# Modulation portions of the second layer's mixer at even distances in TensorE's order

## The chip, the cores and the metric

One Trainium2 chip, one core. The time is device microseconds (us) of one launch of the program, from its runs on the chip; lower is better. The engines are named as in the profile: PE (TensorE, matrix multiplication), PEld (its weight loads), DVE (VectorE), ACT (ScalarE), POOL (GpSimd), SP (SyncE, here the queue that issues most DMAs).

## The reference

Two transformer layers (`DEPTH = 2`) over 256 tokens `x` and 256 context tokens, width 1024, all in float32. Each layer takes six modulation vectors from the condition, runs a mixer (a gated recurrence, neighbourhood attention and windowed attention with a sink), and a mixture of 16 experts. In the last layer only the 256 tokens of `x` go on behind the mixer.

```python
def ada_mod(cond, w, b):
    m = (jax.nn.silu(cond) @ w + b)[..., None, :]
    return jnp.split(m, 6, axis=-1)

for l in range(DEPTH):
    last = l == DEPTH - 1
    sh1, sc1, g1, sh2, sc2, g2 = ada_mod(c, w_ada[l], b_ada[l])
    csh1, csc1, cg1, csh2, csc2, cg2 = ada_mod(c_ctx, w_ada[l], b_ada[l])
    h = x * (1.0 + sc1) + sh1
    hc = ctx * (1.0 + csc1) + csh1
    y, yc = mixer(h, hc, w_in[l], ..., w_out[l], not last)
    x = layer_norm(alpha * x + g1 * y, ln1_g[l], ln1_b[l])
    h2 = x * (1.0 + sc2) + sh2
    ...
    f = moe(h2.reshape(-1, d), w_router, router_bias, w_gate[l], w_up[l], w_down[l]).reshape(x.shape)
    x = layer_norm(alpha * x + g2 * f, ln2_g[l], ln2_b[l])
```

## The kernel before

Every float32 product with a large weight is made of three fast products: a weight piece is split into a high part (a cast on ACT, L294) and a low part (a subtraction on DVE, L304), and the tokens are kept as high and low parts in the regions A, B and C. The split weights go in turn into the regions S and T, so a projection of 128 columns (`proj`, L432) is 24 matrix multiplications out of S or out of T, and the next piece can be split into a region only when the projection before last has read it.

The second layer's mixer (`mixer(1)`) is a set of Python generators that `weave` steps in turn. A rate says how many steps a generator makes in a round. The rounds only say in which order instructions are put into the program; a scheduler then orders each engine's instructions by that order, by priorities and by when it expects their operands. On the chip each engine follows its own order strictly. There are three weaves in this mixer, called the first, second and third window below:

- first: projections (`proj`), the neighbourhood attention of two head pairs (`ux(0, 1)`, `heads_x`), and portions of modulation (`fills(n[0])`);
- second: the recurrence of the first head pair (`hgrn(1, 0)`), projections, `fills(n[1])`;
- third: the recurrence of the second head pair (`hgrn(1, 1)`), projections, windowed attention (`ux(2, 3)`), `fills(n[2])`.

Behind them come the last attention heads woven with the output projection (`outproj`, `op` in the rows, L727), the layer norm, the router and the experts.

A portion of modulation (`fill`, then `ada`) makes two of the 24 blocks of `w_ada`. Its two weight pieces of 1 MB are loaded by POOL (L404) into the two buffers of `aring`, so the pieces of one portion can be loaded only when the portion before has read its own. Then follow 2 x 16 matrix multiplications on PE (`ada`, L411, 32 columns wide, so four stand side by side in the array), a copy on ACT (`vt`, L414), four transposes on PE (`adaT`, L417), and a reduction and two additions on DVE (L419, L424). When the last block of a layer is there, `vectors` makes the router's scaled weights on DVE (L664 to L679, L684), one small product on PE (`rb`, L683), and writes four vectors to DRAM over ACT's queue (`vd`, L687); SP loads them back (L690), and the layer norm's first multiplication (L800) takes the first of them. The portions are made in a fixed order: 14 in the first layer, 6 in the second, here called portions 1 to 6.

`heads_x` makes scores (`S`, L1117), subtracts maxima on DVE (L1122, L1125, L1127), exponentials on ACT (L1129), scales by the sums on DVE (L1137), transposes on PE (`pt`, L1140), copies on ACT (L1141), and multiplies by the values (`py`, L1147). `hgrn` makes seven groups of products on 128 x 128 blocks (`lev`, L999), each behind multiplications on DVE (L1029 to L1032, L989), then transposes of its keys (`kT`, L1049), state products (`dS`, L1056), outputs (`oT`, L1074, L1077) and a norm (`rms`, L1082).

The accumulators are PSUM banks of two pools: three ("d") for `proj`, `pt`, `py`, `kT` and others by `BANKS`, five ("m") for the rest, `ada`, `adaT`, `S`, `lev` and `rb` among them.

```python
FILLS = ((4, 5, 4, 1), (3, 2, 1, 0))
RATES = ((1, 2, 1, 2, 1, 1, 1, 1, 1, 1, 1, 2, 1, 1, 1, 2),
         (1, 2, 2, 2, 1, 1, 1, 1, 2, 3, 1, 1, 1, 1, 1, 3))
```

`FILLS[1]` gives the portions of each call site of the second layer, `RATES[1]` the rates (entries 2, 6 and 10 are those of `fills`).

Of the kernel before, what the change touches and what calls it, by code (L numbers as in the profile page):

```python
# [41 lines left out]
BANKS = {"proj": "d", "first1": "d", "first5": "d", "op1": "d", "xtp": "d", "nT1": "d", "rot": "d", "kT": "d",  # L42
         "pt": "d", "py": "d", "pos": "d", "hgt": "d", "hT": "d", "lt0": "d"}
SPLITC = 6
FILLS = ((4, 5, 4, 1), (3, 2, 1, 0))
EARLY = 6
TAILS = (4, 2)
BANKS1 = {"gu": "d", "hgt": "d", "dn": "m", "hT": "m", "sl": "m"}
ACC = "mmmd"
RATES = ((1, 2, 1, 2, 1, 1, 1, 1, 1, 1, 1, 2, 1, 1, 1, 2),  # L50
         (1, 2, 2, 2, 1, 1, 1, 1, 2, 3, 1, 1, 1, 1, 1, 3))
PRIO = {"hgrn": 0, "x": 200, "c": 0, "op": 0, "ln": 30}

C_ID, C_BLK, C_ROT = 0, 128, 256
# [136 lines left out]
class _Builder:  # L191
# [340 lines left out]
    def mixer(self, l):  # L532
# [48 lines left out]
        def fills(n):  # L581
            for _ in range(n):
                self.fill()
                yield

        def weave(*gs):
            live = list(gs)
# [17 lines left out]
        self.aring = [self.E[2], self.E[3]]  # L605
        n = FILLS[l]
        r = RATES[l]
        self.have.update(COLS[l][:6 + 2 * l])
        weave((pj(6 + 2 * l, 12), r[0]), (ux(0, 1), r[1], "x"), (fills(n[0]), r[2]))
        if l == 0 and not self.general:  # L610
            self.Yd = self.dram([2 * NT, D], "Yd0")
            self.behind(nc.vector.memset(self.Sd, 0.0), self.lasts[1])
            for i in range(2 * NT * D // (512 * P)):
                nc.sync.dma_start(self.Yd[:, :].rearrange("(p r) d -> p (r d)", p=P)[:, i * 512:(i + 1) * 512], self.Sd)
        weave((self.hgrn(l, 0), r[3], "hgrn"), (pj(12, 16), r[4]), (uc(0, 1), r[5], "c"), (fills(n[1]), r[6]))
        for _ in pj(16, 17):
            pass
        weave((self.hgrn(l, 1), r[7], "hgrn"), (pj(17, 22), r[8]), (ux(2, 3), r[9], "x"), (fills(n[2]), r[10]))
        self.direct = True
        cs = range(1 if last else 2)  # L620
# [1604 lines left out]
```

## Time and profile before

| | |
|---|---|
| time, median of 3 runs | 1170.52 us |
| lowest and highest of them | 1166.29 and 1172.93 us |
| the profiled execution's own time | 1173.01 us |
| its span, first to last instruction | 1171.0 us |
| PE busy in the span | 1072.6 us (92%) |
| DVE busy | 744.6 us (64%) |
| ACT busy | 527.1 us (45%) |
| POOL busy | 127.8 us (11%) |
| second layer's mixer, from portion 1 to the end of the output projection | 744.7 to 911.7 us |

The span is that of one execution under the profiler. A row of the timeline gives the start in the span, the time in us, the engine, the source line, the operation, out<-in, the shape and the number of instructions merged into the row; in brackets stands how long the engine sat idle before, and what ended that. Matrix multiplications overlap each other, so the starts of consecutive rows tell more than their times. A short wait of some hundredths of a microsecond is not printed. Rows of stretches (A:B) give for each engine the busy time and, in brackets, the instructions, then the clock that was granted to PE (1.00 is the full 2.4 GHz), the share of the DMA engines and their rate.

### The profile page before, as it was taken

To read this page: it belongs to the slowest core of one execution; us is meant where nothing else is said; L and a number is where in the kernel's file an instruction comes from. 1 tells how busy PE (TensorE), PEld (TensorE's weight loads), DVE (VectorE), ACT (ScalarE), POOL (GpSimd) and SP (SyncE) were. 2 spreads that over 40 slices of the span, in tenths; PEclk is the share of its full clock that TensorE was granted. 3 is DMA by queue.
4 is the path that set the end of the run, shared out by engine and by line. 5 is a ranking of instruction groups with operands and counts; after the bars stand their busy time and mean duration, and the time that the engine had idled before them with its cause. 6 is when DMAs were issued, how large, how long until landed. Compare 5 with 4: busy or idle time off the path is not lost.

```text
span 1171.0 us, 18720 instructions
## 1 busy us (share of the span) xinstructions
PE 1072.6 (92%) x7041; PEld 701.6 (60%) x7041; DVE 744.6 (64%) x1703; ACT 527.1 (45%) x872; POOL 127.8 (11%) x136
## 2 busy tenths in 40 slices
PE   5999999999995999999999968999999499999994
PEld 3776766665674777677644458667766444544451
DVE  3456687767689899788723586578786842222224
ACT  2363443437553677678633354543456511111113
POOL 0000011100000133334310000001000000000000
PEclk8999999999996799999999989999999699999997
DMA  9757666653366799799999951555528579999993
GB/s 376 261 210 263 261 225 233 232 194 127 126 246 237 242 358 358 276 362 384 368 406 415 408 205 72 180 181 216 181 71 332 200 283 422 420 423 422 421 422 155
DMA packets 55202, 327.14 MB, mean 279 GB/s; under 512 B 9467, under 2 KB 9723, under 8 KB 19776
## 3 DMA queue, kind: packets, MB, share of 16 engines
q1 hardware_dynamic: 44080, 275.60, 61.0%
q0 software_dynamic: 9152, 50.10, 11.5%
q8 instruction: 57, 0.93, 0.3%
q10 hardware_dynamic: 1872, 0.16, 0.1%
q14 instruction: 41, 0.34, 0.1%
HBM read 316.53 MB, written 13.09 MB: 281 GB/s over the span
## 4 chain that ended last, share of the span: by engine, by line
PE 74%; DVE 14%; ACT 4%; DMA 3%; issue 3%; POOL 1%; SPq 0%; DVEq 0%; ACTq 0%; POOLq 0%
PE proj L432 13%; PE gu L185 9%; PE gu L1647 7%; PE dn L185 4%; PE dn L1647 4%; PE op L727 4%; PE gu L1638 4%; PE first L432 3%; DMA G<-in_w_ada_dram 3%; PE ada L411 3%; PE pt L1140 2%; PE acc L185 2%; PE hgt L185 2%; PE dn L1638 2%; PE S L1117 2%
## 5 line engine op out<-in xcount | busy, mean ns | idle before, releaser
L294 ACT CAST S<-G 128x1024 fp32r<-128x1024 f32 (+2 forms) x83 | 79.3, 959 | 83.1 <-PE proj L432 52.9
L294 ACT CAST T<-G 128x1024 fp32r<-128x1024 f32 (+2 forms) x79 | 78.1, 994 | 85.0 <-PE proj L432 56.1
L304 DVE TENSOR_TENSOR S<-G,S 128x1024 fp32r<-128x1024 f32 (+2 forms) x75 | 85.8, 1147 | 45.4 <-ACT S L294 43.5
L304 DVE TENSOR_TENSOR T<-G,T 128x1024 fp32r<-128x1024 f32 (+2 forms) x69 | 82.4, 1199 | 40.8 <-ACT T L294 40.4
L185 PE MATMUL gu<-G,C 128*64 128x512 f32 (+2 forms) x608 | 105.9, 494 | 0.7 <-ACT C L1620 0.7
L432 PE MATMUL proj<-A,T 128*128 128x512 f32 (+1 forms) x336 | 97.3, 363 | 1.5 <-ACT T L294 1.0
L432 PE MATMUL proj<-A,S 128*128 128x256 f32 (+1 forms) x336 | 90.2, 347 | 1.3 <-DVE S L304 0.9
L1970 DVE SCALAR_TENSOR_TENSOR vt<-dn,slot,con 128x512 f32<-128x512 f32 x17 | 12.8, 751 | 98.6 <-PE dn L185 98.5
L185 PEld LDWEIGHTS gu<-G,C 128*64 128x64 f32 (+2 forms) x608 | 37.2, 127 | 55.2 <-issue 47.2
L432 PEld LDWEIGHTS proj<-A,T 128*128 128x128 f32 x336 | 59.7, 189 | 16.7 <-issue 4.6
L432 PEld LDWEIGHTS proj<-A,S 128*128 128x128 f32 x336 | 59.7, 195 | 11.5 <-issue 3.1
L1971 ACT CAST S<-vt 128x512 fp32r<-128x512 f32 x17 | 10.5, 618 | 98.8 <-DVE vt L1970 98.8
L1647 PE MATMUL gu<-C,A 128*128 128x512 f32 (+3 forms) x180 | 49.7, 408 | 1.9 <-DVE C L304 1.8
L1647 PE MATMUL gu<-T,A 128*128 128x512 f32 (+3 forms) x174 | 47.8, 405 | 3.3 <-POOL T L302 2.2
L404 POOL DMA_DIRECT2D G<-in_w_ada_dram x40 | 21.9, 549 | 259.1 <-PE ada L411 174.2
L185 PE MATMUL dn<-G,A 128*64 128x512 f32 (+2 forms) x224 | 46.8, 594 | 0.4 <-ACT A L1620 0.4
L1590 POOL DMA_INDIRECT G<-h2d,idx x16 | 22.6, 1410 | 220.6 <-DVE oh L1574 140.3
L294 ACT CAST C<-G 128x1024 fp32r<-128x1024 f32 x38 | 39.8, 1047 | 12.8 <-PE gu L1647 8.2
L1129 ACT ACTIVATE G<-G,nm 128x512 f32<-128x512 f32 x48 | 34.4, 719 | 21.3 <-DVE nm L1127 10.8
L1638 PE MATMUL gu<-G,C 128*64 128x512 f32 x192 | 43.0, 595 | 0.0
L989 DVE TENSOR_TENSOR G<-G 128x256 f32<-128x256 f32 x112 | 42.6, 419 | 0.6
L411 PE MATMUL ada<-G,sT 128*32 128x256 f32 x640 | 40.3, 383 | 1.9 <-DMA G<-in_w_ada_dram 1.9
(477 smaller groups left out, 2398.8 us busy)
## 6 DMA issues: line engine op xcount, KB each, us to landing
G<-in_w_gate_dram SPq DMA_DIRECT2D x62, 1024.0 KB, 9.3
G<-in_w_up_dram SPq DMA_DIRECT2D x60, 1024.0 KB, 8.1
G<-in_w_down_dram SPq DMA_DIRECT2D x60, 1024.0 KB, 11.4
G<-in_w_ada_dram POOLq DMA_DIRECT2D x40, 1024.0 KB, 6.9
G<-in_w_in_dram SPq DMA_DIRECT2D x22, 1024.0 KB, 8.7
G<-in_w_out_dram SPq DMA_DIRECT2D x12, 1024.0 KB, 6.6
G<-in_w_ada_dram SPq DMA_DIRECT2D x8, 1024.0 KB, 15.8
G<-vd SPq DMA_DIRECT2D x11, 512.0 KB, 3.7
```

The costliest lines, as they stand in the source:

```text
L185: return self._then(self.b.nc.tensor.matmul(*a, **k))
L294: self.lasts = [self.nc.scalar.copy(hi, raw)]
L304: self.lasts.append(sub(lo, raw, v))
L411: nc.tensor.matmul(pb[g:g + 32, i * 256:(i + 1) * 256], self.sT[:, kb, :], w[i][:, kb * 256:(kb + 1) * 256], start=kb < 4, stop=kb >= 4, t ...
L432: self.nc.tensor.matmul(pb[:, t], a[:, c], m, start=first and n == 0 and i == 0, stop=last and n == len(kbs) - 1 and i == 2)
L727: nc.tensor.matmul(pbs[tb][h], a, w[j][h], start=n == 0 and i == 0, stop=n == KB - 1 and i == 2)
L989: mul = lambda o, v: tt(o, o, v.to_broadcast([P, n, c]), op=OP.mult)
L1117: nc.tensor.matmul(pb, qT[r, qb * P:(qb + 1) * P], kT[r, :], start=True, stop=True)
L1129: nc.scalar.activation(Pt, Pt, AF.Exp, scale=-1.0, bias=m, accum_out=ls[:, i:i + 1])
L1140: nc.tensor.transpose(pt[:, k * P:(k + 1) * P], Ps[i][:, k * P:(k + 1) * P], self.ident)
L1638: self.pe.matmul(pb[t], h[0][:, g + i], w[o // PIECE][:, o % PIECE:o % PIECE + 512], start=g == 0, stop=g + m == nk, tile_position=(0, i * ...
L1647: nc.tensor.matmul(pbs[j][:cap], h[a][:, k], ws[b][:, c], start=k == 0 and q == 0, stop=k == nk - 1 and q == 2)
```

## The change

The six portions of the second layer's mixer are dealt 2, 2, 2, 0 to the four call sites in place of 3, 2, 1, 0. The generator `fills` yields `GAPS[l]` times behind each portion: once in the first layer, as before, and twice in the second, so that there a round without a portion stands behind each. The rate of `fills` in the second layer's first window goes from 2 steps a round to 1.

```diff
-FILLS = ((4, 5, 4, 1), (3, 2, 1, 0))
+FILLS = ((4, 5, 4, 1), (2, 2, 2, 0))
+GAPS = (1, 2)
...
 RATES = ((1, 2, 1, 2, 1, 1, 1, 1, 1, 1, 1, 2, 1, 1, 1, 2),
-         (1, 2, 2, 2, 1, 1, 1, 1, 2, 3, 1, 1, 1, 1, 1, 3))
+         (1, 2, 1, 2, 1, 1, 1, 1, 2, 3, 1, 1, 1, 1, 1, 3))
...
         def fills(n):
             for _ in range(n):
                 self.fill()
-                yield
+                for _ in range(GAPS[l]):
+                    yield
```

No instruction is added or removed on PE, DVE, POOL or SP; ACT gets two more loads of its function table in this mixer. In the changed kernel's rows the source lines are one higher up to the generator and two higher behind it. The first layer's order stays as it was.

The first place is PE in the first window. Before, portion 3 (`ada_6081`) stands in two halves around four projection products, behind the products with the values (`py`) of the first head pair:

```order
L432 MATMUL proj_6110<-A_114,S_117 128x256
L1147 MATMUL py_6138<-G_72 64x256 x8
L411 MATMUL ada_6081<-G_72,sT_85 32x256 x8
L432 MATMUL proj_6110<-B_115,S_117 128x256
L432 MATMUL proj_6110<-A_114,S_117 128x256 x2
L432 MATMUL proj_6110<-B_115,S_117 128x256
L411 MATMUL ada_6081<-G_72,sT_85 32x256 x8
```

Now, portion 2 (`ada_6102`) stands whole behind that projection, and the second half of the second head pair's scores behind it:

```order
L433 MATMUL proj_6050<-A_114,S_117 128x256
L412 MATMUL ada_6102<-G_72,sT_85 32x256 x16
L433 MATMUL proj_6130<-A_114,T_118 128x512
L433 MATMUL proj_6130<-B_115,T_118 128x512
L433 MATMUL proj_6130<-A_114,T_118 128x512 x2
L418 MATMUL adaT_6121<-con_81,vt_6119 128x128
L1119 MATMUL S_6159<-G_72 128x512
L1119 MATMUL S_6164<-G_72 128x512
L418 MATMUL adaT_6121<-con_81,vt_6119 128x128 x3
```

So only one portion of three is left ahead of that projection, the second stands behind it in one piece, and the third has gone on into the second window.

The second place is PE in the second window, between the second group of `lev` rows (eight of them) and the third. Before, with the last rows of a 512-column projection ahead:

```order
L432 MATMUL proj<-A,T 128x512 x2
L432 MATMUL proj<-C,T 128x512
L432 MATMUL proj<-A,T 128x512
L411 MATMUL ada<-G,sT 32x256 x16
L432 MATMUL proj<-A,S 128x512
L432 MATMUL proj<-B,S 128x512
L432 MATMUL proj<-A,S 128x512 x2
L417 MATMUL adaT<-con,vt 128x128 x4
L999 MATMUL lev<-G 128x128 x8
```

Now:

```order
L433 MATMUL proj<-A,T 128x512 x2
L433 MATMUL proj<-C,T 128x512
L433 MATMUL proj<-A,T 128x512
L1001 MATMUL lev<-G 128x128 x8
L433 MATMUL proj<-A,S 128x512
```

So a portion, its transposes and four projection products no longer stand between the two groups; the portion stands behind the next projection.

The third place is PE in the third window. Before, the last portion (`ada_6708`, portion 6) stands whole, early, ahead of a 512-column projection:

```order
L432 MATMUL proj_6671<-A_114,S_117 128x256
L953 MATMUL vT_6700<-con_81,vt_6668 128x128 x4
L411 MATMUL ada_6708<-G_72,sT_85 32x256 x16
L432 MATMUL proj_6771<-A_114,T_118 128x512
L432 MATMUL proj_6771<-B_115,T_118 128x512
```

Now portion 5 stands there, and portion 6 (`ada_6920`) begins two projections later, between `lev` and the windowed attention's transposes, with nine of its sixteen rows:

```order
L1001 MATMUL lev_6828<-G_72 128x128
L1001 MATMUL lev_6829<-G_72 128x128
L412 MATMUL ada_6920<-G_72,sT_85 32x256 x9
L1142 MATMUL pt_6809<-con_81,G_72 128x128 x4
L1142 MATMUL pt_6816<-con_81,G_72 128x128 x4
```

and ends, one projection further on, in three more pieces:

```order
L963 MATMUL rot_6872<-G_72,con_81 128x256
L412 MATMUL ada_6920<-G_72,sT_85 32x256 x2
L963 MATMUL rot_6878<-G_72,con_81 128x256
L1142 MATMUL pt_6885<-con_81,G_72 128x128 x4
L1142 MATMUL pt_6892<-con_81,G_72 128x128 x4
L412 MATMUL ada_6920<-G_72,sT_85 32x256 x2
L1149 MATMUL py_6898<-G_72 64x256 x8
L412 MATMUL ada_6920<-G_72,sT_85 32x256 x3
L418 MATMUL adaT_6939<-con_81,vt_6937 128x128 x4
L685 MATMUL rb_6964<-posr_6958,onef_490 128x2x16
L1001 MATMUL lev_6973<-G_72 128x128
L1001 MATMUL lev_6974<-G_72 128x128
```

So the portion is spread over the attention of the third window, and the later `lev` rows, which stood between `pt` and `py`, come behind it, as do the second half of the attention's scores.

## Rows read from the trace of the kernel before

**Rows 1.** The page: busy time of an engine (share of the span) and its instructions.

```profile
PE 1072.6 (92%) x7041; PEld 701.6 (60%) x7041; DVE 744.6 (64%) x1703; ACT 527.1 (45%) x872; POOL 127.8 (11%) x136
```

**Rows 2.** Stretches of the mixer: first window, second, its end, third, output projection.

```profile
744.70:784.70 40.00, 37.93 (x289) 25.48 (x288) 26.01 (x78) 20.59 (x37) 3.19 (x6) 1.00 0.54 190
784.70:828.00 43.30, 43.29 (x315) 33.18 (x315) 36.96 (x94) 15.55 (x24) 5.64 (x9) 1.00 0.51 190
828.00:840.40 12.40, 12.40 (x101) 10.00 (x100) 8.56 (x25) 5.21 (x7) 0.00 (x0) 1.00 0.78 274
840.40:876.00 35.60, 32.96 (x218) 20.82 (x217) 29.98 (x90) 19.63 (x45) 3.01 (x4) 1.00 0.28 93
876.00:911.70 35.70, 34.97 (x170) 22.70 (x168) 23.80 (x52) 22.00 (x40) 0.00 (x0) 1.00 0.91 330
```

**Rows 3.** Timeline of PE in the first window: a half portion, and the waits.

```profile
748.87 1.13 PE L1140 MATMUL pt<-con,G 128*128 128x128 f32 x8 [0.66 <-ACT G L915]
...
751.84 1.07 PE L411 MATMUL ada<-G,sT 128*32 128x256 f32 x16
...
762.44 1.07 PE L411 MATMUL ada<-G,sT 128*32 128x256 f32 x16 [0.33 <-DMA G<-in_w_ada_dram]
...
771.86 0.66 PE L1140 MATMUL pt<-con,G 128*128 128x128 f32 x4 [1.01 <-DVE G L1137]
```

**Rows 4.** Timeline of ACT in the first window: a split, a table load and its neighbour.

```profile
745.37 1.04 ACT L294 CAST S<-G 128x1024 fp32r<-128x1024 f32 x1
746.43 1.28 ACT L914 ACT_TABLE_LOAD   x1
747.73 0.60 ACT L914 ACTIVATE G<-proj 128x512 f32<-128x512 f32 x1
```

**Rows 5.** Timelines of PE and DVE in the second window.

```profile
788.62 1.16 PE L999 MATMUL lev<-G 64*128 64x128 f32 x16
789.71 0.50 PE L432 MATMUL proj<-A,T 128*128 128x512 f32 x1
...
794.02 2.12 PE L411 MATMUL ada<-G,sT 128*32 128x256 f32 x32
...
795.11 0.28 DVE L1032 TENSOR_TENSOR G<-G 128x128 f32<-128x128 f32 x1
```

**Rows 6.** Timeline of PE: portion 6, and three waits of the third window.

```profile
828.60 1.93 PE L411 MATMUL ada<-G,sT 128*32 128x256 f32 x32
...
843.55 0.49 PE L999 MATMUL lev<-G 64*128 64x128 f32 x2 [0.48 <-DVE nm L1122]
...
847.99 0.46 PE L999 MATMUL lev<-G 64*128 64x128 f32 x2 [0.71 <-DVE ls L1097]
...
861.56 0.63 PE L1140 MATMUL pt<-con,G 128*128 128x128 f32 x4 [0.35 <-DVE G L1137]
```

**Rows 7.** Timeline of DVE: two small reductions, a maximum in the third window, the layer norm.

```profile
810.00 0.37 DVE L679 TENSOR_REDUCE posr<-tmp 128x16 f32<-128x128 f32 x1
...
832.62 0.19 DVE L419 TENSOR_REDUCE adar<-adaT 128x8 f32<-128x32 f32 x1 [0.49 <-PE adaT L417]
...
857.11 0.75 DVE L1122 CUSTOM_DVE_ANT_0 G<-S,con,nsink 128x512 f32<-128x512 f32 x1
...
908.77 0.69 DVE L800 TENSOR_TENSOR tmp<-op,G 128x512 f32<-128x512 f32 x1 [0.59 <-PE op L727]
```

**Rows 8.** Issues on SP's queue.

```profile
838.46 0.81 SPq L690 DMA_DIRECT2D G<-vd  x2
...
870.74 0.33 SPq L1771 DMA_DIRECT2D G<-in_w_gate_dram  x1
```

**Rows 9.** Stretches ahead of the mixer, where PE paused.

```profile
676.00:680.00 4.00, 0.00 (x0) 0.00 (x0) 2.75 (x5) 3.97 (x7) 0.00 (x0) 0.98 1.01 425
680.00:684.00 4.00, 2.20 (x10) 1.96 (x11) 2.31 (x9) 1.41 (x3) 0.00 (x0) 0.50 0.64 266
684.00:688.00 4.00, 3.29 (x17) 3.01 (x15) 4.00 (x8) 2.48 (x7) 0.00 (x0) 0.67 0.38 113
```

## The prediction, made before the changed kernel ran

> **What bounds the kernel now.** I read the page first: PE is busy for 92% of the span, DVE for 64% [rows 1]. That is an average over stages, so next came the stretches of the second layer's mixer [rows 2], where the reader should subtract PE's busy time from each stretch's length. In the first window PE waits 40.00 - 37.93 = 2.07 us, in the second 0.01, in the 12.4 us behind it nothing, in the third 2.64, in the output projection 0.73: 5.45 us in 167 us, at a granted clock of 1.00 throughout. The portions are PE work which is done either way. So spacing them can win little more than these 5.45 us, and the question is which waits go and where new ones come up. The timeline names them. In the first window they are 0.66 us for ACT, 0.33 us for a weight piece of portion 3 and 1.01 us for DVE's scaled exponentials [rows 3]. In the third they are many short ones behind DVE, the largest 0.48, 0.71 and 0.35 us [rows 6]; DVE itself is busy 29.98 of 35.60 us there [rows 2].
>
> The noise first: with runs before from 1166.29 to 1172.93 us, a difference of about 0.5%, 5.85 us, is what a measurement of this kernel can tell from no change. The sum below is made against the profiled execution's own 1173.01 us, 2.5 us above the median of 1170.52; I carry the difference over to the median.
>
> **Term A, the first window, -0.9 us.** Of the three portions here two were cut into halves. A half took 1.07 us, a whole one takes 1.93 [rows 3, 6], so undoing the cut of portion 2 gives 2 x 1.07 - 1.93 = 0.2 us, and portion 3 gives the same where it goes, uncut: 0.4 in all. The load that portion 3 waited for leaves PE's path: each portion's pieces are now loaded while a projection or more runs, so the 0.33 us go. The wait of 0.66 us lies ahead of the first difference in PE's order and stays. The wait of 1.01 us is DVE's: it belongs to the second head pair's softmax, of which two scores are now made earlier and two later. PE has 17 projection products between the later two and the transposes, and DVE has about as much to do as before; I take half of the wait away, 0.5, with all of it or nothing as bounds. Against that, ACT's cast of the next weight piece now stands ahead of the last copy of the transposed exponentials, and products behind wait for it. Such a cast takes 1.04 us [rows 4]; most of it runs beside products with the first copies, and I charge 0.3, between 0 and 1.0. Sum: -0.4 - 0.33 - 0.5 + 0.3 = -0.9; bounds -2.5 (all 2.07 us of waiting and the 0.4), and +0.3 with nothing of the 0.5 won and the whole cast charged (-0.4 - 0.33 + 1.0).
>
> The two added table loads are on ACT, which is busy 20.59 of 40 us in this window [rows 2]. A load took 1.28 us, and the operation behind it began 0.02 us after it: 746.43 + 1.28 = 747.71 against 747.73 [rows 4]. So ACT gets 2.6 us of work. One load runs under the projection behind the first two exponentials, the other while PE still makes the later scores, and I cost them at nothing. If that cover went, they would lengthen the 1.01 us wait by up to one load, 1.28. The Trainium skill has another price: the page "ScalarE: Activation LUTs", section "What ACT_TABLE_LOAD costs", adds a drain of about 1.38 us to each load, some 2.66 us a switch. By that the two would be an estimated 5.3 us of ACT, and the term up to 1.4 us worse, were the second load's drain to lie in front of the later exponentials; the row shows no such gap, and the sum goes by the row.
>
> **Term B, the second window, +0.8 us.** Portion 5, which began at 794.02, no longer stands between the second and the third group of `lev` products. The second group began at 788.62, and the projection behind it at 789.71, 1.09 us later; it ran to 794.02 [rows 5]. With the portion gone, PE comes to the third group 794.02 - 788.62 = 5.4 us after the second began, and does its first half in 0.55 us. But the second half needs DVE's multiplication that ended at 795.11 + 0.28 = 795.39 [rows 5], 6.8 us after the second group began, and DVE's work in between hangs on that group. So PE waits some 6.8 - 5.95 = 0.8 us where it did not wait. The bounds are 0 (DVE a little earlier) and 1.5 (a little later). Portion 4 now stands ahead of the keys' transposes, which keep PE busy while ACT copies the portion's sums; it costs its own work, which is counted once.
>
> **Term C, the third window, -0.9 us.** Portion 6 leaves a place where PE had no wait, 828.60 [rows 2, 6]: 1.93 us and four transposes, about 0.5 by the like of them [rows 3], 2.4 in all. It goes into the stretch from 840.4 to 876.0, in which PE follows DVE. If that stretch is paced by DVE, its length stays what it was plus what DVE gets: the reduction, the router's vectors and additions that move along, one of 0.37 us and five of about 0.2 like the row of 0.19 [rows 7], together 1.4. So -2.4 + 1.4 = -1.0. Cutting the portion in four costs changes of shape, 0.2 each as with the halves, 0.6 in all; in return the later `lev` rows stand in fewer, longer groups. Two of them alone took 0.49 us, sixteen in a row 1.09, 0.07 each [rows 5, 6]; three groups fewer give back 3 x 0.3 = 0.9. Net -0.3, and I give 0.4 back for the second half of the scores, which now come behind the portion, so that PE has only `lev` rows to do until their softmax is ready. Sum: -0.9. Bounds: -3.4, if the waits of the third window and of the output projection, 2.64 + 0.73, all vanish; +3.0 by the rival below.
>
> The rest is costed at nothing, with its cover. The router's vectors are written some 20 us later, so SP's loads of them, issued at 838.46, go to about 860 [rows 8]; they are needed when the layer norm starts, at 908.77 [rows 7]. Two pieces of the output weights use the portions' buffers and stand just ahead of them in SP's order. The experts' weights behind were first issued at 870.74 [rows 8], so the queue has some ten microseconds to spare before it holds them up. POOL's loads for portions 5 and 6 stand behind its memsets, a projection or more ahead of their use.
>
> **Sum:** -0.9 + 0.8 - 0.9 = -1.0 us: 1172.0 on the profiled execution, 1169.5 on the median. Bounds: -2.5 + 0 - 3.4 = -5.9 and 0.3 + 1.5 + 3.0 = +4.8.
>
> **The rivals.** *The chains through DVE end late.* Behind portion 6 PE meets, in this order, transposes that need the second scores' softmax, two groups of `lev` and the keys' transposes, all of which wait for DVE. Before, the second scores' maxima began at 857.11 and their transposes at 861.56 [rows 6, 7], 4.45 us, and PE had other rows to put between. Now it has twelve `lev` products, 12 x 0.07 = 0.9 us: a wait of 3.5. ACT's copy of the portion's sums adds about 0.6, like the row of 0.60 [rows 4], the keys' transposes perhaps as much as the longest wait for DVE seen, 1.01 [rows 3], and the 0.48 ahead of the portion stays: 5.6 us against 2.64, +3.0. With nothing won in the first window and 0.8 lost in the second that is +3.8, 1174.3. It speaks for it that DVE has 84% of this window; against it, that the moved work fills part of each wait. It decides once the keys' transposes begin over 2.4 us later in the window than now.
>
> *The same, and the clock falls: slower.* Where PE did nothing from 676 to 680, it was granted 0.50 and then 0.67 in the next two stretches of 4 us [rows 9]; 0.50 is the 1.2 GHz level. Were the new waits to join into one pause, 8 us at these clocks would lose 4 x 0.5 + 4 x 0.33 = 3.3 us: 3.8 + 3.3 = +7.1, 1177.6. The Trainium skill, page "TensorE: Matmul & The Clock Gate", section "HAM oscillation — how this bites in real kernels", speaks against any order that lets PE pause, since the clock drops behind long pauses. The pauses I expect are shorter than the one in the row, and in the mixer the clock stayed at 1.00 through all waits [rows 2]; hence a low chance.
>
> *The portions cover every wait: faster.* If the portion in the third window fills PE's waits and delays nothing, both windows come to their bounds: -2.5 - 3.4 = -5.9, 1164.6. It needs DVE's chain to take none of the added 1.4 us, and PE to wait nowhere else.
>
> *PE is full either way.* The order changes as it says, but waits only change places: 0, 1170.5. The time alone can't tell this from my forecast.
>
> **How the numbers follow.** My forecast and "full either way" together have 0.60; the late chains 0.18 (inside 0.5%, on the slow side); these with the clock 0.11; all covered 0.11, of which 0.10 ends beyond 0.5%, and 0.01 of the late chains ends beyond it on the other side. So faster 0.10, same 0.78, slower 0.12. The range runs from 1163.5, the covered case and a microsecond of noise, to 1176.0, the late chains and somewhat more; it leaves out the clock's case and a little at the other end.
>
> **What would show it.** In the first window no wait for a weight piece, and from portion 1 to where the window ended about 36.5 us, 40 less portion 3 and term A. In the second a wait of about 0.8 us inside the third `lev` group. In the third one or two waits of over a microsecond behind the second scores' softmax or at the keys' transposes, and the stretch longer by 1 to 2 us. The clock at 1.00 throughout, and all that follows the output projection shifted as a whole. I am wrong if the third window grows by over 5 us, if the clock leaves 1.00 before the output projection ends, or if the experts start later than the layer norm does.

## The result, and the profile after

The changed kernel took 1176.45 us, the median of ten runs (1172.31 to 1180.2), against 1169.87 for ten runs of the kernel before (1166.29 to 1177.13): a ratio of 1.0053, 95% interval 1.0031 to 1.0074. That is some 6 us slower, half a microsecond beyond the upper end of the range, where the forecast was a gain of one. Twelve more runs of the same kernel gave 1174.22 us and 1.0039 (1.0022 to 1.0055), so some 4.5 to 6 us are lost.

The busy line of the page first, to be held against [rows 1]: PE's share fell by a point.

```profile
PE 1076.6 (91%) x7041; PEld 703.9 (60%) x7041; DVE 744.4 (63%) x1703; ACT 529.5 (45%) x874; POOL 129.0 (11%) x136
```

Then the stretches of the mixer, cut at the same places of the work as [rows 2], except that the first window now ends without portion 3 and that the third holds portion 6:

```profile
743.80:781.10 37.30, 35.99 (x256) 24.71 (x255) 27.33 (x79) 22.52 (x38) 2.12 (x4) 1.00 0.46 170
781.10:824.50 43.40, 42.63 (x315) 33.31 (x315) 34.52 (x87) 15.55 (x24) 6.21 (x9) 1.00 0.46 170
824.50:836.80 12.30, 12.30 (x99) 9.75 (x98) 8.34 (x23) 5.21 (x7) 1.06 (x2) 1.00 0.68 257
836.80:879.50 42.70, 36.81 (x259) 23.43 (x258) 31.60 (x97) 20.13 (x46) 3.11 (x4) 0.96 0.41 136
879.50:916.10 36.60, 35.84 (x166) 23.46 (x167) 23.97 (x52) 22.21 (x40) 0.00 (x0) 0.95 0.88 318
```

PE waits 1.31 us in the first window (2.07 before), 0.77 in the second (0.01), nothing in the stretch behind it, 5.89 in the third (2.64), and 0.76 in the output projection (0.73). The third window is 7.1 us longer, although DVE has only 1.6 us more to do in it. And the granted clock leaves 1.00 in the last two rows, as it did nowhere in [rows 2].

To see where the 7.3 us between the two spans lie, I use five marks that both kernels pass: the start of portion 1, the first `rms` product behind it (the end of the first half of the heads), the first transpose of the layer norm (`nT`), the first expert's `gu` products, and the first `hgt` behind them. PE's timeline, the kernel before (portion 1 starts at 744.71):

```profile
817.15 0.59 PE L1082 MATMUL rms<-G,con 128*128 128x256 f32 x2
911.74 0.68 PE L823 MATMUL nT<-con,G 128*128 128x128 f32 x4
939.41 7.09 PE L185 MATMUL gu<-G,C 128*64 128x512 f32 x32 [0.73 <-ACT C L1620]
946.49 0.25 PE L185 MATMUL hgt<-oh,A 128*128 128x64 bf16 x3
```

PE's timeline of the changed kernel, with these marks and the waits that the prediction spoke of (source lines stand one or two higher than before):

```profile
743.76 1.93 PE L412 MATMUL ada<-G,sT 128*32 128x256 f32 x32
...
770.72 0.66 PE L1142 MATMUL pt<-con,G 128*128 128x128 f32 x4 [0.30 <-DVE G L1139]
...
774.92 1.94 PE L1149 MATMUL py<-G 128*64 128x256 f32 x14 [0.35 <-ACT G L1143]
...
791.90 0.71 PE L1001 MATMUL lev<-G 64*128 64x128 f32 x8 [0.77 <-DVE G L1034]
...
813.65 0.59 PE L1084 MATMUL rms<-G,con 128*128 128x256 f32 x2
...
843.12 1.48 PE L412 MATMUL ada<-G,sT 128*32 128x256 f32 x18 [0.55 <-ACT G L956]
...
853.72 0.63 PE L412 MATMUL ada<-G,sT 128*32 128x256 f32 x6
855.11 0.66 PE L418 MATMUL adaT<-con,vt 128*128 128x128 f32 x4 [0.75 <-ACT vt L415]
...
856.16 1.03 PE L1119 MATMUL S<-G 64*128 64x512 f32 x4
...
861.55 2.82 PE L1142 MATMUL pt<-con,G 128*128 128x128 f32 x15 [2.81 <-DVE G L1139]
...
884.90 1.79 PE L1119 MATMUL S<-G 64*128 64x512 f32 x4 [0.72 <-DVE nm L1124]
...
916.11 0.68 PE L825 MATMUL nT<-con,G 128*128 128x128 f32 x4
...
943.17 9.63 PE L186 MATMUL gu<-G,C 128*64 128x512 f32 x32 [0.73 <-ACT C L1622]
...
952.80 0.25 PE L186 MATMUL hgt<-oh,A 128*128 128x64 bf16 x3
```

From portion 1 to `rms` it is 69.89 us against 72.44, with one portion less; from `rms` to `nT` 102.46 against 94.59, with one more; from `nT` to the `hgt` behind the first `gu` 36.69 against 34.75. The experts behind, 225.5 against 224.5, add 1.0, and portion 1 starts 0.95 earlier, which the change has no part in: -0.95 - 2.55 + 7.87 + 1.94 + 1.0 = 7.31. So the loss starts behind `rms`, in the third window and the output projection.

What is late there shows in DVE and ACT around the second head pair's softmax. DVE:

```profile
855.39 0.42 DVE L647 TENSOR_TENSOR C<-G,A 128x256 fp32r<-128x256 f32 x1 [1.44 <-ACT A L646]
...
857.22 0.75 DVE L1124 CUSTOM_DVE_ANT_0 G<-S,con,nsink 128x512 f32<-128x512 f32 x1 [0.74 <-PE S L1119]
...
860.62 1.67 DVE L1139 TENSOR_SCALAR G<-G,ls 128x512 f32<-128x512 f32 x4
```

and ACT:

```profile
854.47 0.59 ACT L415 COPY vt<-ada 128x512 f32<-128x512 f32 x1 [0.27 <-PE ada L412]
854.95 0.41 ACT L646 CAST A<-G 128x256 fp32r<-128x256 f32 x1
```

Read these rows in the order of the work. Portion 6 ends on PE at 853.72 + 0.63; ACT copies its sums until 855.06; PE transposes them from 855.11; only then, at 856.16, come the last scores of the second head pair, which before had been made by 851.5. DVE, with nothing else to do, waits for them (0.74 us, after 1.44 for a cast that stood behind the same copy on ACT) and starts their maxima at 857.22. From the maxima to the transposes it is 4.33 us, as before (4.45). But PE has few rows to put between: the `py` products that stood there before, 1.94 us, it has already done. So it waits 2.81 us where it waited 0.35 [rows 6].

The clock, last. Stretches of 2 us behind that wait and at the head of the output projection (PE busy, granted clock, DMA share, GB/s):

```profile
860.00:862.00 2.00, 0.45 (x4) 1.00 0.70 233
862.00:864.00 2.00, 1.86 (x13) 0.75 0.90 287
864.00:866.00 2.00, 2.00 (x7) 0.50 0.03 8
866.00:868.00 2.00, 2.00 (x20) 0.90 0.00 0
884.00:886.00 2.00, 1.28 (x4) 1.00 0.89 377
886.00:888.00 2.00, 2.00 (x7) 0.72 0.24 49
888.00:890.00 2.00, 2.00 (x9) 0.50 0.91 299
890.00:892.00 2.00, 2.00 (x9) 0.92 0.87 311
```

Twice PE had waited in the 2 us before, and twice the clock fell to the 1.2 GHz level: 2 x (0.25 + 0.50 + 0.10) = 1.7 us of full clock lost, and 2 x (0.28 + 0.50 + 0.08) = 1.7. But the second of these waits is not the change's doing. The kernel before has it too, and its clock stayed at 1.00 there:

```profile
881.31 1.79 PE L1117 MATMUL S<-G 64*128 64x512 f32 x4 [0.73 <-DVE nm L1122]
```

The first expert's 32 `gu` products, 9.63 us against 7.09, are another 2.5: behind the router's pause the clock stood at 0.50 until 948, where in the kernel before it was back at 1.00 by 940. Nor is that shown to be the change's doing: in a second profile of each kernel the changed one took 7.09 us for them and the one before 9.30. So of the 7.87 us between `rms` and `nT`, 3.4 are clock and 4.5 are the portion with its waits. A portion by itself is 2.4 to 2.5 us of PE, which leaves some 2.0.

### The profile page after: what moved, and what is told of

The parts are those of the page before. It is cut to its first block, busy times and chain, and to the rows that moved or that the text cites. A ratio compares the mean times of both kernels' runs of the same rounds, so it can differ in the third digit from the quotient of the medians.

```text
span 1178.3 us, 18719 instructions
## 1 busy us (share of the span) xinstructions
PE 1076.6 (91%) x7041; PEld 703.9 (60%) x7041; DVE 744.4 (63%) x1703; ACT 529.5 (45%) x874; POOL 129.0 (11%) x136
## 4 chain that ended last, share of the span: by engine, by line
PE 75%; DVE 13%; ACT 5%; DMA 3%; issue 3%; POOL 1%; SPq 0%; ACTq 0%; DVEq 0%; POOLq 0%
PE proj L433 12%; PE gu L186 9%; PE gu L1649 8%; PE dn L186 4%; PE op L729 4%; PE dn L1649 4%; PE gu L1640 4%; PE first L433 3%; PE ada L412 3%; DMA G<-in_w_ada_dram 2%; PE pt L1142 2%; PE hgt L186 2%; PE dn L1640 2%; PE py L1149 2%; PE acc L186 2%
## 5 line engine op out<-in xcount | busy, mean ns | idle before, releaser
L186 PE MATMUL gu<-G,C 128*64 128x512 f32 (+2 forms) x608 | 108.5, 503 | 0.7 <-ACT C L1622 0.7
```

What stands on the lines that cost most here:

```text
L186: return self._then(self.b.nc.tensor.matmul(*a, **k))
```

## The experiments

One table for all, since they are read together. Each kernel ran twelve times, beside 17 to 35 runs of the kernel before (for the changed kernel ten and ten). "Clock" is the mean over its runs of the clock granted in the span. "Portion 1 to `nT`" is from its profile, and behind it the same less what was lost at the half clock (each slice of 1 us counts its PE time by what its clock lacks, so that waits inside a slow stretch are corrected a little too much). In the last column the runs are compared at one clock: over the 270 runs that list it (the table's 154 and 116 of the runs of the kernel before beside them), a line with one slope for all kernels says 0.75 us for each 0.001 of mean clock, and the column gives the height of each kernel's line against that of before (within about 0.9 us either way; how far chance goes, the first row shows, where twelve runs of the kernel before stand against its other 116). Idle work in a wait may raise the mean clock without saving time, so the column may be too high where some was added.

| kernel | median us | ratio to before, 95% | clock | portion 1 to `nT` | at one clock |
|---|---|---|---|---|---|
| before, again | 1171.28 | 1.0014 (0.9992 to 1.0036) | 0.9576 | 172.5 / 166.1 | +0.8 |
| the changed kernel | 1176.45 | 1.0053 (1.0031 to 1.0074) | 0.9553 | 172.3 / 168.9 | +3.5, with the next |
| the changed kernel, again | 1174.22 | 1.0039 (1.0022 to 1.0055) | 0.9579 | 171.0 / 169.3 | |
| third window alone | 1174.01 | 1.0021 (1.0 to 1.0042) | 0.9597 | 172.2 / 170.6 | +4.1 |
| first window alone | 1173.09 | 1.0013 (0.999 to 1.0037) | 0.9552 | 171.4 / 166.6 | +0.4 |
| late fold | 1174.78 | 1.0041 (1.0016 to 1.0067) | 0.9543 | 172.6 / 167.5 | +2.5 |
| pause filled | 1173.58 | 1.0015 (0.9997 to 1.0034) | 0.9578 | 171.0 / 169.4 | +2.2 |
| pause in before | 1175.58 | 1.0039 (1.002 to 1.0058) | 0.9562 | 172.2 / 168.8 | +3.6 |
| four rounds between | 1176.75 | 1.006 (1.0041 to 1.0079) | 0.9542 | 174.3 / 167.5 | +3.4 |
| two pauses filled | 1174.42 | 1.0034 (1.0014 to 1.0054) | 0.9579 | 170.2 / 170.2 | +3.4 |
| before, filled | 1171.38 | 1.0005 (0.9987 to 1.0023) | 0.9592 | 173.5 / 167.1 | +1.5 |
| idle work ahead of experts | 1172.55 | 1.0015 (0.9998 to 1.0033) | 0.9592 | 166.7 / 166.7 | +2.2 |
| two, three and one, spaced | 1170.24 | 0.9995 (0.9978 to 1.0012) | 0.9580 | 167.0 / 167.0 | -0.3 |

The profile of before that the prediction read has 167.0 us from portion 1 to `nT`, all at 1.00.

**The windows apart.** Two kernels, each with one half of the change. In these the gap is a number for each window:

```diff
-FILLS = ((4, 5, 4, 1), (2, 2, 2, 0))
+FILLS = ((4, 5, 4, 1), (3, 1, 2, 0))
-GAPS = (1, 2)
+GAPS = ((1, 1, 1, 1), (1, 2, 2, 1))
-         (1, 2, 1, 2, 1, 1, 1, 1, 2, 3, 1, 1, 1, 1, 1, 3))
+         (1, 2, 2, 2, 1, 1, 1, 1, 2, 3, 1, 1, 1, 1, 1, 3))
```

> First window as before (three portions, portion 3 among them), one portion in the second, portions 5 and 6 with two rounds apart in the third, whose order on TensorE is that of the changed kernel. Theory L (the third window carries the loss: portion 6 ends in a place where the second head pair's last scores stand behind it, PE then waits 2.8 us for DVE, and the clock falls twice behind that wait): 5 to 7 us above before, some 1175 to 1177, with the wait of over 2.5 us, a stretch at 0.50 within 5 us behind it and the first expert's gate/up near 9.6 us. Rival E (the two early windows lose it, by the third scores, the two added table loads and portion 4's place, and everything behind is only displaced): within 2 us of before, 1168 to 1172, clock 1.00 to the end of the output projection.

The other keeps the changed kernel's rates:

```diff
-FILLS = ((4, 5, 4, 1), (2, 2, 2, 0))
+FILLS = ((4, 5, 4, 1), (2, 3, 1, 0))
-GAPS = (1, 2)
+GAPS = ((1, 1, 1, 1), (2, 1, 1, 1))
```

> First window as in the changed kernel (two portions, spaced), three in the second, one in the third, whose order on TensorE is that of before. Theory L: no more than 1 us from before, or up to 1 us faster by what the first window gained (0.25 us) and a covered wait in the second, 1168.5 to 1170.5; clock 1.00 from the first window to the output projection's end. Rival E: 5 to 7 us above before.

The times settle little: 1.0021 and 1.0013 overlap, as the runs spread over 10 and 13 us. Theory L's 5 to 7 us were too much for the first. The traces do tell them apart: with the third window alone the wait of 2.81 us is there, one fall of the clock behind it, and 170.6 us from portion 1 to `nT`; with the first alone there is no such wait and it is 166.6. At one clock that is +4.1 and +0.4. Two of L's signs did not come: the first experts' products took 7.09 us with the third window alone, not near 9.6, and with the first alone the clock did not stay at 1.00 but stood at 0.50 from 847 to 856. And some of the 170.6 us was lost before the third window: from portion 1 to `rms`, with as many portions, this kernel takes 71.07 us, the changed one 69.89.

**The scores ahead of portion 6's transposes.** The copy, the transposes and the sums of a portion come a round after its products in the third window (with a gap of one there, so that portion 6's products keep their round):

```diff
-                self.ada(*a)
+                fold = self.ada(*a)
+                if late:
+                    yield
+                fold()
```

> The changed kernel, with the copy and the four transposes of portions 5 and 6 a round later than their products: the last scores of the second head pair then stand ahead of portion 6's transposes on TensorE. Theory L1 (the scores are late since they stand behind portion 6's copy and transposes, and that makes the long wait): the scores start about 1.5 us earlier against portion 6's end, the wait for the scaled exponentials falls from 2.8 to about 1.3 us, no stretch at 0.50 behind it, and the time is 1169 to 1172. Rival L2 (DVE's own work paces the softmax, wherever the scores stand): the wait stays at 2.3 us or more and the time at 1174 to 1178.

In its timeline the four score products stand at 849.89, ahead of the transposes at 851.07, and the wait is less than half as long, but a new one stands at the keys' transposes:

```profile
854.97 3.61 PE L1150 MATMUL pt<-con,G 128*128 128x128 f32 x16 [1.22 <-DVE G L1147]
...
864.80 1.39 PE L1059 MATMUL kT<-con,G 128*128 128x128 f32 x6 [2.37 <-issue]
```

So L1 is right about the wait: 1.22 us, as it expected 1.3, and the mixer apart from the clock is 1.4 to 1.8 us shorter than the changed kernel's. It is wrong about the time, and about the clock, which fell behind both waits (855 to 859 and 866 to 872). The runs had a lower mean clock (0.9543), and the new wait was there; how much each gave back is not shown.

**The wait filled.** Twelve transposes whose result nothing reads, in the changed kernel's long wait:

```diff
+                if late and qb == 0 and hh == 0:
+                    dm = self.bank("xtp")
+                    for k in range(12):
+                        nc.tensor.transpose(dm[:, 0:P], Ps[3][:, 0:P], self.ident)
```

> The changed kernel with twelve idle transposes of the last exponentials (nothing reads them) in the long wait of the third window; about 2 us of PE work where PE waited 2.8. Theory C (the pause makes the clock fall, and the fallen clock is most of the loss): no stretch at 0.50 between 862 and 892, the output projection ends some 3 us earlier than in the changed kernel, and the time is 1171 to 1174. Rival D (the clock falls for another reason, or the loss is the late chain itself): both half-clock stretches stay, and the time is 1175 to 1178, the same as the changed kernel or a little above it.

```profile
856.08 1.53 PE L1142 MATMUL xtp<-con,G 128*128 128x128 f32 x12 [1.06 <-ACT G L1131]
857.83 2.21 PE L1146 MATMUL pt<-con,G 128*128 128x128 f32 x15 [0.21 <-DVE G L1143]
```

Of the wait 1.06 + 0.21 us were left, and no slow stretch stood behind it; one stood at 838 to 842 instead, and from portion 1 to `nT` it took as long as in the changed kernel. The time was where C wanted it, but its interval meets that of the changed kernel's second twelve runs, so I tried it at two places, adding six transposes ahead of the scores of the output projection:

> The changed kernel with twelve idle transposes in its long wait, as in the run that filled the pause, and six more in the wait of 0.72 us for the next scores at the head of the output projection. Theory C (clock falls behind these two waits are what the changed kernel loses beyond its late chain, some 2 to 3 us): 1 to 3 us above before, mean clock 0.958 or more, no stretch at 0.50 between 860 and 912. Rival D (filling waits does nothing that lasts; the lower time of the run that filled one pause was chance): 4 to 6 us above before, as the changed kernel is.

Here no stretch was slow from portion 1 to `nT`, and the 170.2 us show the waits and the idle work bare, 3.2 us above before. The time, 1.0034, is the changed kernel's again. And the control, the twelve transposes in the kernel before:

> The kernel before with the same twelve idle transposes in the same place, where TensorE waits only 0.35 us: a control. Theory C: nothing to win there, and the transposes cost what DVE's chain does not cover, 0 to 2 us above before. Rival D (idle transposes help any kernel, by work as such and not by filling this wait): 1.5 to 3 us below before.

It cost nothing that can be measured (1.0005), and its mixer apart from the clock is that of before (167.1 against 167.0). So filling waits neither helps as such nor brings the changed kernel back: the late chain itself remains. That fewer falls of the clock come with filled waits is not shown.

**A wait made in the kernel before.** Six multiplications by 1.0 ahead of the second head pair's scaling, with the same result:

```diff
+                if late and qb == 0 and hh == 0:
+                    for _ in range(6):
+                        nc.vector.tensor_scalar_mul(Ps[i], Ps[i], 1.0)
```

> The kernel before, with six multiplications by 1.0 of a 128x512 piece (0.42 us each, some 2.5 us of DVE) ahead of the second head pair's scaling in the third window: a longer wait on TensorE in the same place, with nothing else of the change. Theory C (the long wait itself costs, by the wait and by a clock that falls behind such a wait more often): a wait of 2 to 3 us there, 3 to 6 us above before, and a mean granted clock over its runs nearer to the changed kernel's 0.955 than to 0.960. Rival D (waits here are made up later, as the output projection has to wait for the same chains anyway): within 1.5 us of before.

```profile
863.13 2.63 PE L1143 MATMUL pt<-con,G 128*128 128x128 f32 x15 [2.77 <-DVE G L1140]
```

A wait of 2.77 us, the clock at 0.57 from 864 to 872, and 1.0039: nothing of the change but its wait, and the same loss. Rival D falls. The mean clock, 0.9562, is lower than the 0.9580 of all 128 runs of the kernel before, which by the slope is 1.3 us of the 4.6; the wait grew by 2.4; some 0.9 stay open.

**The unchanged kernels again.**

> The kernel before, unchanged, so that its granted clock stands beside its time run by run. Both theories expect the time within 0.2% of before. Theory C: the mean clock of its runs lies above the changed kernel's 0.955, at 0.958 or more, and the runs' times follow the clock as closely as those of the changed kernel did. Rival D: a mean clock of 0.955 as well, so that the clock has no part in the difference.

> The changed kernel, unchanged, on the same chip as its variants. Theory L: 3 to 8 us above before (0.3 to 0.7%), mean clock 0.955, and above the variants without the long wait. Rival N (the first ten runs caught the clock low by chance): within 2 us of before, mean clock 0.958 or more.

The kernel before had a mean clock of 0.9576, not quite C's 0.958 (over all its 128 runs it is 0.9580); the changed kernel, in twelve runs, 0.9579, so that here the clock has no part in the difference, and it was still 3 us slower in the median (1174.22 against 1171.28). In the first ten runs it had 0.9553: 0.0026 less, 2.0 us by the slope, which is the difference between the means of the two sets, 1176.6 and 1174.7. All runs together, its mean of 22 lies 4.4 us above that of 128 (1175.6 against 1171.2), and its mean clock 0.0012 lower (0.9567 against 0.9580), which is 0.9 us: the other 3.5 are there at an equal clock. Of these the mixer shows 2 to 3 in the profiles, apart from the clock; where the rest lies stays open. And the kernel before is not free of such falls: in the profile of its twelve runs it ran its third window at the half clock for most of 15 us, which made its mixer as long as the changed kernel's first (172.5 us). The stretch, with the granted clock third from the right:

```profile
839.00:854.00 15.00, 14.24 (x55) 0.54 0.01 5
```

**Portion 6 in the wait itself.** Four rounds between the portions of the third window:

```diff
-GAPS = (1, 2)
+GAPS = ((1, 1, 1, 1), (2, 2, 4, 1))
```

> The changed kernel with four rounds in place of two behind a portion in the third window: portion 6 then stands on TensorE right before the transposes of the second head pair, in the long wait, and the pair's last scores stand ahead of it, inside a projection. Theory L1 (the scores' place behind portion 6 makes the wait): the wait of 2.8 us falls below 1 us, no stretch at 0.50 in the third window, and the time is that of before or lower, 1167 to 1171. Rival L2 (DVE paces the softmax wherever the scores stand, and the wait goes elsewhere, to the sums of portion 6 or the keys' transposes): a new wait of 1.5 us or more behind, time 1173 to 1177.

L1's wait is gone, with real work in it. But as L2 expected, others came up, behind the moved portion and at the output weights:

```profile
864.92 1.15 PE L1051 MATMUL kT<-con,G 128*128 128x128 f32 x6 [1.46 <-DVE G L1040]
...
869.96 0.73 PE L729 MATMUL op<-S,A 128*128 128x512 f32 x2 [1.40 <-DVE S L305]
```

The clock stood at 0.53 from 871 to 882, and this was the slowest kernel of all. Apart from the clock its mixer is 0.5 us longer than before's; the 3.4 us at one clock are more than that explains, and that stays open.

**Idle work ahead of the first experts**, in the kernel before: 20 transposes in layer 1's wait for gathered rows, 24 small products late in layer 2's router:

```diff
+        if i == 0 and not self.native and not self.general:
+            dm = self.bank("xtp")
+            for k in range(20):
+                t = self.nc.tensor.transpose(dm[:, 0:P], self.ident, self.ident)
+                self.behind(t, self.lastsl)
...
+        if l == DEPTH - 1 and not self.general:
+            dm = self.bank("xtp")
+            for k in range(24):
+                nc.tensor.matmul(dm[:, 0:160], self.tri, self.cmp, start=True, stop=True)
```

> The kernel before with idle TensorE work ahead of the first experts: 20 transposes (6 us at the half clock) in layer 1's wait of 6.09 us for the gathered rows, and 24 small products in the last 4 us of layer 2's router wait of 12.69 us. Theory C (a pause is paid at the clock behind it, and work in the pause buys it back): the products behind run at 1.00 from their start; layer 1 has 2 us pieces at 0.50 from 380 to 392 that are PE-busy, so up to 5 us there, and 1 to 2.5 us in layer 2, less what weights and DVE make of it: 3 to 7 us below before, 1164 to 1168. Rival D (the experts wait for their weights and for DVE's splits, not for the clock): within 1.5 us of before.

Between 388 and 392 layer 1's `gu` products ran at 1.00, against 0.50 in the kernel before, but the time did not fall: D. Before 384 they still ran at 0.50, and layer 2's idle products did nothing for the clock, which stood at 0.50 until 933 and at 0.72 from there to 935, when the `gu` began. The DMA engines were busy 0.96 and 0.97 of the stretches 388 to 392 and 392 to 396, so that the weights, I take it, set the pace there; that was not tried by itself. The `gu` of layer 2 took 7.09 us, as before.

**The placement that is left.** Spaced portions in the first and second windows, one in the third:

```diff
-FILLS = ((4, 5, 4, 1), (2, 2, 2, 0))
+FILLS = ((4, 5, 4, 1), (2, 3, 1, 0))
-GAPS = (1, 2)
+GAPS = ((1, 1, 1, 1), (2, 2, 1, 1))
```

> The placement that the earlier runs point to: portions spaced by two rounds in the first and second windows (two and three of them), and a single portion in the third window, whose order on TensorE is that of before. Theory L (the early windows give about nothing, and the whole loss of the change is the third window's second portion): within 2 us of before on equal clock, no wait of over 1.1 us for DVE in the third window, from the first portion to the first transposes of the layer norm 166 to 167.5 us apart from stretches at the half clock, against 168.9 in the changed kernel and 167.0 before. Rival E (the spacing in the early windows costs as well): 169 us or more there, and 3 us or more above before.

```profile
809.76 0.59 PE L1084 MATMUL rms<-G,con 128*128 128x256 f32 x2
...
906.86 0.68 PE L825 MATMUL nT<-con,G 128*128 128x128 f32 x4
```

Portion 1 starts at 739.88. To `rms` it is 69.88 us, as in the changed kernel (69.89); to `nT` 97.10, at 1.00 throughout, against 94.59 before with one portion less. The time is that of before, 0.9995 (0.9978 to 1.0012), an interval that lies wholly below the changed kernel's two. Theory L holds and E falls: what the change does in the first two windows is worth nothing that these runs can tell (-0.3 at one clock, within 0.9), and its loss is the second portion in the third window. No version was measurably faster than before.

## Why the prediction was wrong

The forecast was 1169.5 us; the step that failed is term C, the sign of which was wrong.

- **Terms A and B were right as a sum, and that was luck.** The weight piece's wait is gone, the 1.01 us wait is 0.30, the cast ahead of the last copy costs 0.35 where 0.3 was charged, and the third `lev` group waits 0.77 us where 0.8 was forecast. Portion 1 to `rms` is 2.55 us shorter with one portion (2.4) less: -0.1, and -0.9 + 0.8 = -0.1 was on paper. But the 36.5 us from portion 1 to the first window's end were 37.3, so A gave about nothing, and the second window, with two portions either way, was 43.40 us against 43.30, so B cost 0.1 and not 0.8, although its wait came: PE's busy time there fell by 0.66. What A left out is that the second head pair's scores were cut. Eight of them took 1.92 us in one group (764.53 to 766.45 before, first row); in three groups they take 1.05 + 1.05 + 1.06 = 3.16, each from its start to the next row's:

```profile
764.53 1.99 PE L1117 MATMUL S<-G 64*128 64x512 f32 x8
749.14 1.12 PE L1119 MATMUL S<-G 64*128 64x512 f32 x2
...
750.78 1.12 PE L1119 MATMUL S<-G 64*128 64x512 f32 x2
...
764.91 1.13 PE L1119 MATMUL S<-G 64*128 64x512 f32 x4
```

- **Term C, -0.9, measured about +2.0, before any change of clock.** The sum took the third window as paced by DVE, so that a portion there would cost only DVE's own 1.4 us. But it gave DVE a pace that did not depend on PE's order. Portion 6's tail runs over PE, ACT and PE again, and the last scores stood behind it in PE's order: DVE stood idle 2.18 us there, 1.44 for a cast behind the portion's copy on ACT (0.59 us) and 0.74 for the scores behind its transposes on PE. DVE got 1.6 us more to do in the window, close to the 1.4 on paper, but the window grew by 7.1: 3.25 of waiting, 1.7 of clock, and 2.15 that are about the portion's own 2.4. The 0.4 that I gave back "for the second half of the scores" named the place and was several times too small.
- **The rival of the late chains had mechanism and price.** It put the wait behind the second softmax at 3.5 us (2.81, and 0.41 at the `lev` group ahead of it), ACT's copy at 0.6 (0.75), the stretch at +3.0 (waits 5.89 against 2.64 in the third window, 3.25 more). Its total, +3.8, lies between the 3.5 us at one clock and the 4.6 (0.0039 x 1170) of the second twelve runs. Against it I had held that the moved work fills part of each wait; it was the moved work that made the wait.
- **The rival with the clock gave the number, 1177.6, and in part the reason.** The pauses did not join into one of 8 us; behind a wait of 2.8 us the clock fell in all four profiles that have it (both of the changed kernel, third window alone, pause in before), and that fall cost 1.7 us in the first. With the one behind the wait of 0.7 us, which the kernel before has at full clock, that makes 3.4, where 3.3 stood on paper. My reason for a low chance, that the clock stayed at 1.00 in the mixer through all waits, was read from one execution. In another of the same kernel it did not.
- **What I listed as proof of an error came true**: the clock left 1.00 before the output projection ended. The third window grew by over 5 us, and the output projection's later part was displaced as a whole.

The Trainium skill's rule, on the page "TensorE: Matmul & The Clock Gate", section "HAM oscillation — how this bites in real kernels", that a clock lost in pauses slows the work behind them, agrees with the rows of 862 to 866, behind the wait of 2.81 us. That the change loses by the clock more than by its waits is not shown: with an equal mean clock it was still slower by 3 us.

The two added table loads cost ACT 1.28 us each and no more. The operation behind the first began 0.01 us after its end (751.49 + 1.28 = 752.77), and so it was with the second (757.87 + 1.28 = 759.15, the next at 759.16):

```profile
751.49 1.28 ACT L1131 ACT_TABLE_LOAD   x1
752.78 0.73 ACT L1131 ACTIVATE G<-G,nm 128x512 f32<-128x512 f32 x1
```

The Trainium skill's price, on the page "ScalarE: Activation LUTs", section "What ACT_TABLE_LOAD costs", with a drain of about 1.38 us on top of each load, does not show in these rows.

## What to carry to other kernels

Moving filler work into a stretch that another engine paces is free only if nothing that engine needs stands behind the filler in the issuing engine's order; follow the filler's last product through its copy and transposes, and look at what is queued behind them. Before trusting "the clock stayed full" or a gain of half a per cent, look at the clock of several executions: compare kernels at equal clock, or by stretches that ran at full clock.

## What the runs showed that I had not expected

The run-to-run spread of this kernel is mostly the clock's. Over the 270 runs that list it the time follows the mean granted clock by 0.75 us per 0.001, which is some seven tenths of the variance within a kernel; in the changed kernel's first ten it goes from 1172.31 us at 0.960 to 1180.2 at 0.952. Where the clock falls in the mixer differs between executions of one and the same program: nowhere between portion 1 and `nT` in the first profile of before, most of 839 to 854 in the second; twice in the changed kernel's first profile, once in its second. Three such stretches of 10 to 15 us stand in profiles whose third window has the order of before and no wait over 1 us (the second of before, first window alone, before filled), so that order does not ensure a full clock. So a single profile shows what a wait can cost, not what it costs on average.
